# Output weights and residual with their channel means taken off beforehand, and a layer norm that takes the mean of squares alone

## The chip, the core and the metric

The kernel runs on one core of one Trainium2 chip. Its engines: TensorE (PE; PEld is its weight load), VectorE (DVE), ScalarE (ACT), GpSimd (POOL) and SyncE (SP), and 16 DMA engines that serve queues issued from SP, ACT and POOL. PE multiplies into PSUM; DVE and ACT read PSUM; POOL works on SBUF alone. The metric is the device time in microseconds of one execution.

## What is computed

One layer of a hybrid decoder for a prompt of 1024 tokens and 8 sampled tokens (1032 columns in all). The part that the change touches, cut from the reference:

```python
proj = jnp.einsum('ntd,de->nte', x, P['w_in'])
...
gated = jnp.concatenate([o_A * _silu(z_A), o_B * _silu(z_B), o_C * _silu(z_C), o_D * _silu(z_D)], axis=-1)
out = jnp.einsum('nte,ed->ntd', gated, P['w_out'])
y = _layernorm(ALPHA_DN * x + out, P['ln_g'], P['ln_b'])

def _layernorm(x, g, b):
    mu = jnp.mean(xf, axis=-1, keepdims=True)
    var = jnp.mean(jnp.square(xf - mu), axis=-1, keepdims=True)
    return (xf - mu) * lax.rsqrt(var + LN_EPS) * g + b
```

The mean and the variance go over the 2048 channels of one token. `o_A` is a gated delta rule, `o_B` an RWKV-7 recurrence, `o_C` an attention with forget gates (over the prompt, and over paged caches for the sampled tokens), `o_D` a pooling. `w_out` is 2048 by 2048.

## The kernel before, in words

**Layout.** Channels lie on the 128 partitions and tokens on the columns, so the 2048 channels are 16 tiles of 128 by 1032. A product in fp32 precision is three matmuls of rounded halves (`mm3`, lines 306 to 310): weight and data are each split into a rounded value `hi` and a remainder `lo`.

**Weights.** `weight` and `fetch` (lines 280 to 304) load a piece of 128 by 512 (256 KB) into `raw` (two buffers, on ACT's DMA queue), let ACT cast it to `hi` (line 302) and DVE subtract to get `lo` (line 303). They run up to two pieces ahead of the product that asks, with a high priority. For the output pass pieces 48 to 63 are kept in SBUF (`wkh`, `wkl`), all others go through four rotating buffers.

**Order.** The tile framework schedules the instructions: within each engine it orders them by a modelled timeline and by priority, which is the program's order unless a block raises it, and each engine then takes its own queue strictly in order. The kernel's side work is written as Python generators ("fillers") that are advanced by `fill` (lines 315 to 327): a filler with rate 1.3 gets 1.3 steps at each call. `project` (lines 343 to 361) calls it four times for a tile of the input projection; `drain` runs what is left.

**Stages.** (1) The input projection, 57 tiles of 128 output columns, each 144 matmuls of 344 columns. In `inputs` (lines 854 to 881) come first the tiles of branch B, then, from `self.add(self.start_b(), 1)` on (line 878), the sixteen tiles of branch A, the delta rule; beside them run `post_a` and `prep_a` (lines 385 to 488), and `start_b` (lines 1893 to 1897): the inverses of branch B and its step for the sampled tokens, 44 steps. `inputs_cd` then projects the rest beside the inverses of A and the cached scores (`cached`) and the recurrences (`recurrent`). (2) The attention over the prompt (`mixing`), with the cached values beside it. (3) The output product, one pass for each branch in the order D, B, A, C. The first three (`out_pass`, lines 1699 to 1721) add into sixteen accumulators `y`; the third of them also adds 2^0.25 times the residual, loaded from `in_xT` (lines 1711 to 1714).

**The last pass** (`out_last`, lines 1723 to 1781) takes the columns in three groups of 392, 384 and 256. For each group and each of 16 channel tiles PE first multiplies `mneg` (all entries -16/2048) with a rounded copy of `y[0]` (line 1765), then adds twelve matmuls; this takes off an estimate of the mean. DVE adds the PSUM result into `y` (line 1769) and `y` into a running sum `s1` (line 1775); ACT squares (line 1776); POOL, and in the third group DVE, adds the squares into `s2` (line 1777). PSUM has five buffers for these results. When a group is done, `norm` (lines 1736 to 1754) forms the means of `s1` and `s2` by two matmuls with a constant matrix (line 1741), copies them out, subtracts the squared mean and takes the reciprocal root on ACT (`rsqrt`, lines 1231 to 1235). Then for each channel tile DVE or POOL subtracts the mean (line 1750) and multiplies (line 1751), ACT applies scale and shift (line 1752), and SP stores (line 1753). `norm` of one group is a filler beside the matmuls of the next; that of the third group runs alone at the end.

Of the kernel before, what the change touches and what calls it, by code (L numbers as in the profile page):

```python
# [18 lines left out]
G3 = 344  # L19
# [160 lines left out]
class Kernel:  # L180
# [94 lines left out]
    def weights(self, pool, srcs, pieces, keep=1 << 30):  # L275


        self.wp, self.wsrc, self.wraw, self.wsplit, self.wkeep, self.wn = pool, srcs, {}, {}, keep, pieces
# [7 lines left out]
    def fetch(self, i):  # L286
        nc, p = self.nc, self.wn
        w = 4 // p
        for j in range(i // p, min(i // p + 4, len(self.wsrc))):
# [3 lines left out]
            for n in range(p * j, p * j + p):  # L293
# [8 lines left out]
                nc.scalar.copy(hi, raw)  # L302
                nc.vector.tensor_tensor(lo, raw, hi.bitcast(F32), op=ALU.subtract)  # L303
# [1382 lines left out]

    def gated(self, br, gp, stage):
# [11 lines left out]
    def out_pass(self, i, g, stage):  # L1699
# [3 lines left out]
        for ct in range(16):  # L1703
# [7 lines left out]
            if i == 2:  # L1711
                xr = self.t(stage, [128, N], "ostg")
                nc.sync.dma_start(xr, I["xT"][ct])
                nc.vector.scalar_tensor_tensor(y, xr, ALPHA, y, op0=ALU.mult, op1=ALU.add)
# [8 lines left out]
    def out_last(self, i, g, stage, pool):  # L1723


# [4 lines left out]
        mneg = self.t(pool, [128, 128], "mneg", F32R)  # L1730
        nc.vector.tensor_scalar(mneg, m2k, -16.0, None, op0=ALU.mult)
        yr = self.t(stage, [128, N], "ostg", F32R)
        nc.scalar.copy(yr, self.y[0])
        W = {}

        def norm(s, n, st):
            s1, s2 = st
            sq = self.t(pool, [128, GROUPS[0]], "sq", bufs=2)[:, :n]
            for x in (s1, s2):
                ps = self.ps("b", (128, n))  # L1740
                nc.tensor.matmul(ps, lhsT=m2k, rhs=x, start=True, stop=True)
                nc.vector.tensor_copy(x, ps)
            nc.scalar.activation(sq, s1, AF.Square)
            nc.vector.tensor_tensor(s2, s2, sq, op=ALU.subtract)
            self.rsqrt(s2, s2, self.eps["ln"])
            yield True
            for ct in range(16):
                y = self.y[ct][:, s]
                e = nc.gpsimd if ct * NPOOL[n] % 16 < NPOOL[n] and ct else nc.vector
                e.tensor_tensor(y, y, s1, op=ALU.subtract)  # L1750
# [5 lines left out]
        for n in GROUPS:  # L1756
            s = slice(g0, g0 + n)
            st = [self.t(pool, [128, GROUPS[0]], x, bufs=2)[:, :n] for x in ("s1", "s2")]
            for ct in range(16):
# [5 lines left out]
                nc.tensor.matmul(ps, lhsT=mneg, rhs=yr[:, s], start=True, stop=False)  # L1765
                for j in range(4):
                    self.mm3(ps, hi[:, j], lo[:, j], gh[:, j, s], gl[:, j, s], False, j == 3)
                y = self.y[ct][:, s]
                nc.vector.tensor_tensor(y, y, ps, op=ALU.add)  # L1769
                if ct == 0:  # L1770
                    nc.vector.tensor_copy(st[0], y)
                    nc.scalar.activation(st[1], y, AF.Square)
                else:
                    sq = self.t(pool, [128, GROUPS[0]], "sq", bufs=2)[:, :n]
                    nc.vector.tensor_tensor(st[0], st[0], y, op=ALU.add)  # L1775
# [191 lines left out]
```

## Time and profile before

| | |
|---|---|
| median of 3 runs | 2395.63 us (2390.84 to 2396.36) |
| the profiled execution | 2396.94 us, of which the span of the profile 2395.2 us |
| busy: PE, PEld | 2282.6 us (95%), 2023.0 us (84%) |
| busy: DVE, ACT, POOL | 1364.7 us (57%), 938.4 us (39%), 295.0 us (12%) |
| DMA | 402.44 MB, mean 168 GB/s |
| mean granted clock of PE | 0.979 |

Times in the profile count from the first instruction. Matmuls are pipelined, so that the duration of one is longer than the time from its start to the next one's start. A view of windows gives for each stretch its length, the time in which each engine was busy with the number of its instructions in brackets, the granted clock of PE (1.00 is full speed), the mean busy share of the DMA engines and what they moved. A view of waits gives idle time of an engine ahead of a line's instructions, and what ended it.

### The profile page before, as it was taken

The numbers are of one execution on the slowest core, as the hardware profiler recorded it, in microseconds if no ns is written. First come the engines' busy times: TensorE is split into PE (matmuls) and PEld (weight loads), VectorE is DVE, ScalarE is ACT, GpSimd is POOL, SyncE is SP. The second block draws the span as 40 slices with busy tenths as digits, with TensorE's granted clock in tenths as the row PEclk, the third lists the DMA queues.
The fourth block names the chain that finished last, engine by engine and source line by source line (L and its number), as shares of the span: only waits on it lengthen the run. The fifth ranks groups of instructions, "written<-read, shape, count | busy, mean of one in ns | idle before, by whom it ended". The sixth has DMA issues, their size and how long they took to land. (4 is left out here: it accounts for less than half of the span.)

```text
span 2395.2 us, 47251 instructions
## 1 busy us (share of the span) xinstructions
PE 2282.6 (95%) x17640; PEld 2023.0 (84%) x17640; DVE 1364.7 (57%) x2676; ACT 938.4 (39%) x1853; POOL 295.0 (12%) x408
## 2 busy tenths in 40 slices
PE   8999999999899999999999999999899999999984
PEld 8999999998899999787787877899755578889984
DVE  4665757677576557432222245555578644564598
ACT  5644445434454444121111122454366665211244
POOL 0000000000000000103111121100132110100175
PEclk9999999999999999999999999999999999999997
DMA  6133323545523336778878888653488775683212
GB/s 215 56 100 95 104 85 95 151 106 120 113 81 94 89 107 142 172 187 264 274 250 283 259 273 288 232 161 107 124 260 248 223 282 192 219 304 129 88 63 88
DMA packets 369664, 402.44 MB, mean 168 GB/s; under 512 B 204877, under 2 KB 228350, under 8 KB 368666
## 3 DMA queue, kind: packets, MB, share of 16 engines
q1 hardware_dynamic: 307698, 263.83, 37.3%
q10 hardware_dynamic: 50056, 101.60, 13.9%
q0 software_dynamic: 11680, 33.99, 4.3%
q8 instruction: 139, 2.28, 0.4%
q14 instruction: 91, 0.75, 0.1%
HBM read 314.56 MB, written 84.67 MB: 167 GB/s over the span
## 5 line engine op out<-in xcount | busy, mean ns | idle before, releaser
L308 PE MATMUL pj<-xh,wlo 128*128 128x344 f32 x2688 | 873.1, 326 | 16.7 <-DVE wlo L303 8.6
L309 PE MATMUL pj<-xl,whi 128*128 128x344 f32 x2688 | 871.5, 324 | 0.0
L310 PE MATMUL pj<-xh,whi 128*128 128x344 f32 x2688 | 865.2, 324 | 0.0
L308 PEld LDWEIGHTS pj<-xh,wlo 128*128 128x128 f32 x2688 | 508.1, 189 | 37.1 <-issue 11.4
L309 PEld LDWEIGHTS pj<-xl,whi 128*128 128x128 f32 x2688 | 508.5, 189 | 19.8 <-issue 14.4
L310 PEld LDWEIGHTS pj<-xh,whi 128*128 128x128 f32 x2688 | 507.9, 189 | 16.4 <-issue 13.1
L302 ACT CAST whi<-raw 128x256 fp32r<-128x256 f32 (+1 forms) x504 | 213.0, 424 | 732.6 <-PE pj L310 530.2
L303 DVE TENSOR_TENSOR wlo<-raw,whi 128x256 fp32r<-128x256 f32 (+1 forms) x504 | 226.8, 452 | 365.5 <-ACT whi L302 356.1
L309 PE MATMUL o<-gl,whi 128*128 128x344 f32 x576 | 185.8, 323 | 0.0
L308 PE MATMUL o<-gh,wlo 128*128 128x344 f32 x576 | 184.6, 325 | 0.8 <-ACT gh L1695 0.5
L310 PE MATMUL o<-gh,whi 128*128 128x344 f32 x576 | 185.1, 321 | 0.0
L308 PEld LDWEIGHTS o<-gh,wlo 128*128 128x128 f32 x576 | 107.9, 188 | 21.8 <-DVE y L1720 9.4
L309 PEld LDWEIGHTS o<-gl,whi 128*128 128x128 f32 x576 | 109.0, 189 | 2.3 <-DVE ps L1221 0.9
L310 PEld LDWEIGHTS o<-gh,whi 128*128 128x128 f32 x576 | 109.0, 189 | 0.8 <-issue 0.8
L365 ACT ACTIVATE stg<-pj 128x344 f32<-128x344 f32 x168 | 74.6, 457 | 74.2 <-PE pj L310 73.0
L997 PE MATMUL k<-dkv,dqb 128*32 128x256 f32 x1024 | 88.4, 394 | 15.1 <-DMA dkv<-in_ck 9.0
L1720 DVE TENSOR_TENSOR y<-y,o 128x344 f32<-128x344 f32 x96 | 48.0, 510 | 57.3 <-PE o L310 57.0
L1105 PE MATMUL k<-dkv,dpT 128*8 128x512 f32 x512 | 71.5, 635 | 0.8 <-DMA dkv<-in_cv 0.8
L861 DVE TENSOR_TENSOR cpl<-cpt,cph 128x512 fp32r<-128x512 f32 (+1 forms) x96 | 60.9, 653 | 15.7 <-ACT cph L860 14.9
L308 PE MATMUL o<-gh,wkl 128*128 128x392 f32 (+2 forms) x192 | 63.9, 333 | 0.6 <-DVE wkl L303 0.5
L310 PE MATMUL o<-gh,wkh 128*128 128x392 f32 (+2 forms) x192 | 63.6, 331 | 0.0
L309 PE MATMUL o<-gl,wkh 128*128 128x392 f32 (+2 forms) x192 | 63.3, 330 | 0.0
(597 smaller groups left out, 3321.9 us busy)
## 6 DMA issues: line engine op xcount, KB each, us to landing
dkv<-in_ck SPq DMA_DIRECT2D x256, 256.0 KB
dkv<-in_cv SPq DMA_DIRECT2D x256, 256.0 KB
raw<-in_w ACTq DMA_DIRECT2D x228, 256.0 KB
out_pj<-stg ACTq DMA_DIRECT2D x33, 516.0 KB
bop<-bop SPq DMA_DIRECT2D x16, 1024.0 KB
raw<-in_wo ACTq DMA_DIRECT2D x64, 256.0 KB
aop<-aop SPq DMA_DIRECT2D x16, 768.0 KB
aop<-aost SPq DMA_DIRECT2D x40, 256.0 KB
```

The source lines that it names most:

```text
L302: nc.scalar.copy(hi, raw)
L303: nc.vector.tensor_tensor(lo, raw, hi.bitcast(F32), op=ALU.subtract)
L308: nc.tensor.matmul(ps, lhsT=wlo, rhs=xh, start=start, stop=False)
L309: nc.tensor.matmul(ps, lhsT=whi, rhs=xl, start=False, stop=False)
L310: self.last = nc.tensor.matmul(ps, lhsT=whi, rhs=xh, start=False, stop=stop).ins
L365: self.nc.scalar.activation(dst[:, g * G3:g * G3 + G3], ps[g], func)
L861: nc.vector.tensor_tensor(pl[:, off:], pt[:, off:], ph[:, off:].bitcast(F32), op=ALU.subtract)
L997: nc.tensor.matmul(ps[32 * hp:32 * hp + 32], lhsT=qb[:, hp, b], rhs=kt[:, :, hp], start=b == 0, stop=b == 7)
L1105: mm = lambda i: nc.tensor.matmul(po[32 * i:32 * i + 8], lhsT=pTv[:, c, :, 4 * bg + i], rhs=t[i // 2][:, i % 2], start=False, stop=c == 31)
L1720: nc.vector.tensor_tensor(y[:, s], y[:, s], ps[g], op=ALU.add)
```

## The change

`start_b` gets a third part, `centre`, and its rate goes from 1 to 1.3. `centre` loads all output weights and sums them over the output channels (64 pieces, SP queue and DVE), loads the residual and sums it over its channels (POOL, then two matmuls for each third of the columns), loads it a second time, subtracts the mean (POOL) and stores the result in DRAM (`XC`). The 16 columns `wm` hold minus the means of the weights. When the output weights are split later, `wm` is added: ACT's one cast becomes four activations with a bias, DVE's one subtraction four with a scalar. The third output pass reads `XC` instead of `in_xT`. With that the sum over channels of `y` is zero but for rounding, and the last pass leaves out the `mneg` matmuls, the sum `s1` and everything that came from it.

```diff
@@ fetch
-                nc.scalar.copy(hi, raw)
-                nc.vector.tensor_tensor(lo, raw, hi.bitcast(F32), op=ALU.subtract)
+                if self.wless:
+                    m = self.wless(n)
+                    for k in range(4):
+                        nc.scalar.activation(hi[:, k], raw[:, k], AF.Identity, bias=m[:, k:k + 1])
+                        nc.vector.scalar_tensor_tensor(lo[:, k], raw[:, k], m[:, k:k + 1], hi[:, k].bitcast(F32),
+                                                       op0=ALU.add, op1=ALU.subtract)
+                else:
...
@@ new
+    def centre(self, keep):
+        nc = self.nc
+        self.wm = self.t(keep, [128, 16], "wm")
+        with self.tc.tile_pool(reuse_waits="tile", name="cen", bufs=1) as pool:
+            part = self.t(pool, [128, 16, 16], "wpart")
+            load = lambda n: self.t(pool, [128, N], "cin", bufs=2)[:, 0:n]
+            for ct in range(16):
+                for br in range(4):
+                    r = load(512)
+                    nc.sync.dma_start(r.rearrange("p (k m) -> p k m", k=4), self.I["wo"][ct][:, 4 * br:4 * br + 4])
+                    nc.vector.reduce_sum(part[:, 4 * br:4 * br + 4, ct], r.rearrange("p (k m) -> p k m", k=4), axis=AX.X)
+                yield 1
+            nc.vector.reduce_sum(self.wm, part, axis=AX.X)
+            nc.vector.tensor_scalar(self.wm, self.wm, -1.0 / D, None, op0=ALU.mult)
+            xs = self.t(pool, [128, N], "csum")
+            for k in range(16):
+                r = xs if k == 0 else load(N)
+                nc.sync.dma_start(r, self.I["xT"][k])
+                if k:
+                    nc.gpsimd.tensor_tensor(xs, xs, r, op=ALU.add)
+                if k % 4 == 3:
+                    yield 1
+            m2k = self.t(pool, [128, 128], "cone", F32R)
+            nc.vector.tensor_scalar(m2k, self.onec.to_broadcast([128, 128]), 1.0 / D, None, op0=ALU.mult)
+            for g in range(3):
+                s = slice(g * G3, g * G3 + G3)
+                hi, lo = (self.t(pool, [128, N], "cin", F32R, bufs=2)[:, 0:G3] for _ in range(2))
+                nc.scalar.copy(hi, xs[:, s])
+                nc.vector.tensor_tensor(lo, xs[:, s], hi.bitcast(F32), op=ALU.subtract)
+                ps = self.ps("b", (128, G3))
+                nc.tensor.matmul(ps, lhsT=m2k, rhs=lo, start=True, stop=False)
+                nc.tensor.matmul(ps, lhsT=m2k, rhs=hi, start=False, stop=True)
+                nc.vector.tensor_copy(xs[:, s], ps)
+            yield 1
+            for k in range(16):
+                r = load(N)
+                nc.sync.dma_start(r, self.I["xT"][k])
+                nc.gpsimd.tensor_tensor(r, r, xs, op=ALU.subtract)
+                nc.sync.dma_start(self.XC[k], r)
+                if k % 2:
+                    yield 1
@@ out_pass
-                nc.sync.dma_start(xr, I["xT"][ct])
+                nc.sync.dma_start(xr, self.XC[ct])
@@ out_last
-        mneg = self.t(pool, [128, 128], "mneg", F32R)
-        nc.vector.tensor_scalar(mneg, m2k, -16.0, None, op0=ALU.mult)
-        yr = self.t(stage, [128, N], "ostg", F32R)
-        nc.scalar.copy(yr, self.y[0])
...
-        def norm(s, n, st):
-            s1, s2 = st
-            sq = self.t(pool, [128, GROUPS[0]], "sq", bufs=2)[:, :n]
-            for x in (s1, s2):
-                ps = self.ps("b", (128, n))
-                nc.tensor.matmul(ps, lhsT=m2k, rhs=x, start=True, stop=True)
-                nc.vector.tensor_copy(x, ps)
-            nc.scalar.activation(sq, s1, AF.Square)
-            nc.vector.tensor_tensor(s2, s2, sq, op=ALU.subtract)
-            self.rsqrt(s2, s2, self.eps["ln"])
+        def norm(s, n, s2):
+            ps = self.ps("b", (128, n))
+            nc.tensor.matmul(ps, lhsT=m2k, rhs=s2, start=True, stop=True)
+            self.rsqrt(s2, ps, self.eps["ln"])
...
-                e.tensor_tensor(y, y, s1, op=ALU.subtract)
                 e.tensor_tensor(y, y, s2, op=ALU.mult)
...
-                nc.tensor.matmul(ps, lhsT=mneg, rhs=yr[:, s], start=True, stop=False)
                 for j in range(4):
-                    self.mm3(ps, hi[:, j], lo[:, j], gh[:, j, s], gl[:, j, s], False, j == 3)
+                    self.mm3(ps, hi[:, j], lo[:, j], gh[:, j, s], gl[:, j, s], j == 0, j == 3)
...
-                    nc.vector.tensor_copy(st[0], y)
...
-                    nc.vector.tensor_tensor(st[0], st[0], y, op=ALU.add)
@@ inputs
-            self.add(self.start_b(), 1)
+            self.add(self.start_b(cp), 1.3)
@@ start_b
+        yield from self.centre(keep)
```

## Rows read from the trace of the kernel before

**Rows 1.** Windows of the end: length; PE, PEld, DVE, ACT, POOL; PEclk, DMA share, GB/s

```profile
2245.30:2284.80 39.50, 37.99 (x208) 37.01 (x209) 29.03 (x47) 14.75 (x28) 12.47 (x12) 1.00 0.29 94
2284.80:2331.80 47.00, 40.45 (x215) 38.93 (x214) 45.03 (x56) 20.83 (x37) 36.92 (x31) 0.93 0.19 69
2331.80:2369.50 37.70, 29.55 (x213) 28.11 (x211) 36.29 (x58) 16.28 (x31) 25.02 (x21) 0.86 0.23 85
2369.50:2395.20 25.70, 1.92 (x4) 0.80 (x4) 17.60 (x30) 11.92 (x24) 12.10 (x14) 0.58 0.24 82
```

**Rows 2.** The waits of PE from 2280 us to the end: us, times, longest

```profile
PE o L1765 <- DVE y L1769: 14.7, 6, 5.3
PE b L1741 <- DVE s L1777: 8.2, 1, 8.2
```

**Rows 3.** The chain that ended last, 2246 to 2275 us: start, us, what

```profile
2250.62 3.06 DMA raw<-in_wo
...
2270.25 0.70 DVE wkl L303
```

**Rows 4.** PE's timeline at the start of the third group: start, us

```profile
2331.77 0.28 PE L1765 MATMUL o<-ostg,mneg 128*128 128x256 f32 x1
...
2333.30 0.28 PE L1765 MATMUL o<-ostg,mneg 128*128 128x256 f32 x1
```

**Rows 5.** DVE's groups by shape, 2245 us on: busy us, mean ns | idle before

```profile
L1750 DVE TENSOR_TENSOR y<-y,s 128x392 f32<-128x392 f32 x9 | 11.1, 1301 | 0.0
L1751 DVE TENSOR_TENSOR y<-y,s 128x384 f32<-128x384 f32 x7 | 9.1, 1356 | 0.0
...
L1777 DVE TENSOR_TENSOR s<-s,sq 128x256 f32<-128x256 f32 x15 | 7.9, 525 | 0.1
...
L1769 DVE TENSOR_TENSOR y<-y,o 128x256 f32<-128x256 f32 x16 | 6.4, 410 | 0.5 <-PE o L310 0.5
```

**Rows 6.** Groups of ACT's instructions by line and shape, the whole run

```profile
L302 ACT CAST whi<-raw 128x256 fp32r<-128x256 f32 x456 | 183.2, 403 | 583.2 <-PE pj L310 530.2 <-DMA raw<-in_w 20.9 <-DMA dkv<-in_ck 9.9
...
L302 ACT CAST whi<-raw 128x512 fp32r<-128x512 f32 x48 | 29.7, 619 | 149.3 <-PE o L310 130.6 <-DMA raw<-in_wo 10.3 <-DVE y L1720 6.2
...
L555 ACT ACTIVATE bot<-bot,par 128x512 f32<-128x512 f32 x8 | 5.8, 723 | 1.2 <-DVE bot L554 1.2
```

**Rows 7.** The timeline of the tail, from 2379 us: start, duration

```profile
2379.59 1.22 PE L1741 MATMUL b<-s,m2k 128*128 128x256 f32 x2 [8.23 <-DVE s L1777]
...
2381.84 0.51 ACT L1234 ACTIVATE s<-s,epsln 128x256 f32<-128x256 f32 x1 [4.06 <-DVE s L1744]
...
2382.83 6.82 DVE L1751 TENSOR_TENSOR y<-y,s 128x256 f32<-128x256 f32 x9 [1.02 <-ACT s L1235]
```

**Rows 8.** The stores of line 394: ns min/median/max, first and last start

```profile
L394 SPq DMA_DIRECT2D out_pj<-stg x12: 338/360/702, 471.7 to 836.3; - x12
```

**Rows 9.** Windows of earlier stretches

```profile
0.00:36.00 36.00, 27.42 (x165) 27.42 (x166) 22.55 (x36) 21.60 (x30) 1.24 (x6) 1.00 0.87 298
520.00:540.00 20.00, 20.00 (x128) 19.72 (x126) 19.31 (x51) 8.06 (x17) 0.00 (x0) 1.00 0.17 54
700.00:880.00 180.00, 180.00 (x1476) 174.02 (x1475) 109.11 (x193) 86.31 (x169) 0.91 (x4) 1.00 0.31 86
880.00:960.00 80.00, 79.39 (x680) 76.48 (x679) 54.76 (x129) 32.80 (x64) 4.82 (x7) 1.00 0.65 147
1080.00:1500.00 420.00, 405.26 (x4304) 321.09 (x4304) 123.98 (x253) 68.96 (x153) 80.39 (x148) 0.98 0.84 271
```

**Rows 10.** Groups of DVE's and POOL's instructions by line and shape, the whole run

```profile
L789 DVE TENSOR_REDUCE cmx<-b 128x1 f32<-128x512 f32 x24 | 16.4, 686 | 3.8 <-PE b L785 3.5
...
L912 POOL TENSOR_TENSOR cnum<-cnum,cz 128x1024 f32<-128x1024 f32 x4 | 9.8, 2456 | 0.3
```

**Rows 11.** POOL's timeline, 890 to 900 us

```profile
898.38 1.81 POOL L1210 MEMSET ivB<- 128x2048 f32 x1 [98.61 <-DVE am L417]
```

**Rows 12.** The waits of PE, 540 to 1010 us

```profile
PE k L1182 <- DMA ivB<-ut: 4.6, 1, 4.6
```

More of the change, by code (lines that the diff above doesn't have):

```diff
@@ L273, in load_x, with weights @@
             nc.vector.tensor_tensor(self.xl[k], r, self.xh[k].bitcast(F32), op=ALU.subtract)
-    def weights(self, pool, srcs, pieces, keep=1 << 30):
+    def weights(self, pool, srcs, pieces, keep=1 << 30, less=None):
+        self.wless = less
         self.wp, self.wsrc, self.wraw, self.wsplit, self.wkeep, self.wn = pool, srcs, {}, {}, keep, pieces
@@ L301, in fetch @@
                 raw = self.wraw[j][:, w * (n % p):w * (n % p) + w]
-                nc.scalar.copy(hi, raw)
-                nc.vector.tensor_tensor(lo, raw, hi.bitcast(F32), op=ALU.subtract)
+                if self.wless:
[5 more added lines that the diff above has]
+                else:
+                    nc.scalar.copy(hi, raw)
+                    nc.vector.tensor_tensor(lo, raw, hi.bitcast(F32), op=ALU.subtract)
                 self.wsplit[n] = hi, lo
@@ L1757, in out_last @@
             s = slice(g0, g0 + n)
-            st = [self.t(pool, [128, GROUPS[0]], x, bufs=2)[:, :n] for x in ("s1", "s2")]
+            s2 = self.t(pool, [128, GROUPS[0]], "s2", bufs=2)[:, :n]
             for ct in range(16):
@@ L1770, in out_last @@
                 if ct == 0:
-                    nc.vector.tensor_copy(st[0], y)
-                    nc.scalar.activation(st[1], y, AF.Square)
+                    nc.scalar.activation(s2, y, AF.Square)
                 else:
                     sq = self.t(pool, [128, GROUPS[0]], "sq", bufs=2)[:, :n]
-                    nc.vector.tensor_tensor(st[0], st[0], y, op=ALU.add)
                     nc.scalar.activation(sq, y, AF.Square)
-                    (nc.gpsimd if ct <= SPOOL[GROUPS.index(n)] else nc.vector).tensor_tensor(st[1], st[1], sq, op=ALU.add)
+                    (nc.gpsimd if ct <= SPOOL[GROUPS.index(n)] else nc.vector).tensor_tensor(s2, s2, sq, op=ALU.add)
                 self.fill()
-            self.add(norm(s, n, st), 1)
+            self.add(norm(s, n, s2), 1)
             g0 += n
@@ L1795, in build @@
         self.UT = tc.dram_tile([4, 16, 32, 32], F32, name="ut")
+        self.XC = tc.dram_tile([16, 128, N], F32, name="xc")
         self.lfd = tc.dram_tile([8, 32, 1024], F32, name="lfd")
@@ L1830, in build @@
                     order = (3, 1, 0, 2)
-                    self.weights(wp, [self.I["wo"][ct][:, 4 * br:4 * br + 4] for br in order for ct in range(16)], 1, 48)
+                    self.weights(wp, [self.I["wo"][ct][:, 4 * br:4 * br + 4] for br in order for ct in range(16)], 1, 48,
+                                 lambda n: self.wm[:, 4 * order[n // 16]:4 * order[n // 16] + 4])
                     with P(name="g1", bufs=1) as g1:
@@ L1891, in inputs_cd, with start_b @@
         self.drain()
-    def start_b(self):
+    def start_b(self, keep):
         yield from self.inverses("B")
```

## The prediction

> **What bounds the kernel now.** I read the span in windows first. TensorE (PE) is busy nearly everywhere except at the end, so the only stretches in which this change can earn time are those where PE waits, and the only way it can lose time is to make PE wait where it does not today. The last 150 us, cut at the ends of the three column groups of the last pass, are [rows 1]: 39.5, 47.0, 37.7 us and a tail of 25.7 us in which PE has almost nothing. The reader should see the DVE column: 45.0 of 47.0 us and 36.3 of 37.7 us. VectorE (DVE), not PE, sets the second and third group. The waits of PE say the same [rows 2]: 14.7 us for the adds of line 1769, because five PSUM buffers are full and DVE is behind. The first group has another limit, the loading and splitting of the sixteen kept weights: DVE is not full there, and the chain of waits goes load, cast, split, next load [rows 3].
>
> **What leaves the end.** (a) PE: 48 matmuls with `mneg`. Thirteen 256-column matmuls lie between two of them, 2331.77 to 2333.30, so one takes 0.118 us [rows 4]; scaled by columns 0.118, 0.177 and 0.18 us, times 16 each, 7.6 us in all. (b) DVE and GpSimd (POOL): the sums `s1`, the subtraction of the mean, and copies. In the second group's time these are fifteen adds and nine subtractions on DVE, the subtractions alone 11.1 us [rows 5]. I then rebuild each stretch.
>
> First group: limited by weights, so (a) is worth nothing here (if it were not, 2.9 us). Each weight is now four pieces on ScalarE (ACT) and four on DVE. A cast takes 0.403 us for 256 columns and 0.619 us for 512; the line through both gives 0.295 us for 128. A bias column adds about 0.1 us (0.723 for 512 with it) [rows 6]. Four pieces are thus 1.2 us (bias free) to 1.6 us (as read) instead of 0.62. DVE no longer has to wait for the whole cast: its last piece follows ACT's by about 0.35 us instead of 0.70 [rows 3], so a pair of weights, with a load of 3.06 us, turns over in about 4.9 us instead of 4.5. Seven pairs: 3 us lost, 2 us back from the adds that no longer stand between. I take 1 us slower; ends 3 us faster and 4 us slower.
>
> Second group: PE needs 16 x 12 x 0.177 = 34 us and 0.8 us for the reduction. DVE keeps its adds and nine multiplications, at most half of its 45.0 us. I take 36 instead of 47.0: 11 us saved (ends 8 and 12).
>
> Third group: PE 16 x 12 x 0.118 = 22.7 us. DVE: 16 adds at 0.410, 15 at 0.525, 7 multiplications at 1.356 [rows 5], 24 us. The two are level, so some wait stays: 27 instead of 37.7, 10.7 us saved (ends 6 and 13).
>
> Tail: add, square and add of the last tile 1.2 us, matmul 1.22, the two activations 1.0 (2381.84 to 2382.83), multiplications 6.82, the last activations and the last store 5.5 (2389.65 to the end) [rows 7], handoffs 0.6: 16.4, I take 17 instead of 25.7. What goes is the backlog of 8.2 us that PE waits for before the last matmul [rows 2] and the copy and subtraction after it. 8.7 us saved (ends 6 and 10).
>
> Sum of the end: 11 + 10.7 + 8.7 - 1 = 29 us, ends 16 and 39.
>
> **What is added in the middle.** Here the work is large, and all of it must hide beside the projections of the delta rule's sixteen tiles. By the stores of line 394 these tiles finish 26 us apart, the first at about 471 us and the last at about 862 [rows 8]; four calls of fill a tile make one each 6.5 us. The new generator has 44 steps before `centre` and 29 in it; at 1.3 a call, 83 steps fit in the 64 calls, so nothing is left for the drain. `centre` starts after 34 calls, at about 690 us.
> - Transfers: 64 of 256 KB, and 48 of 528 KB, 42 MB. The start of the kernel moves 298 GB/s at a share of 0.87; so these are 123 us of all engines, and 700 to 880 us has 0.31 taken, 124 us free [rows 9]. They fill it to the brim. PE's loss beside full queues: 1080 to 1500 us runs at a share of 0.84, with PE 405.3 of 420 us busy, 3.5% idle; 700 to 880 us has no idle at all. 250 us at 3.5% are 9 us. Ends 0 (PE full, as in 700 to 880) and 15 us.
> - DVE: 64 reductions of 512 columns at 0.686 = 44 us [rows 10], some 5 us for the split of the sum. They read tiles that the SP queue loads; with two buffers a load (3.06) and a reduction allow one each 1.95 us, 125 us against the 80 us that the steps give. What stands behind: on DVE the weight splits, for which PE waits; on SP, whose next load waits for a reduction, the operand loads and stores of `prep_a` (lines 407, 440, 485), for which ACT and the stage buffers wait. The splits run up to two weights ahead, which covers single waits.
> - POOL: 15 adds and 16 subtractions of 1032 columns at 2.46 us for 1024 [rows 10], 76 us on an engine that is idle there (0.91 us busy in 180, [rows 9]). DVE pays beside it: nine subtractions of 392 columns next to POOL's took 1.301 us each [rows 5], where one of 512 columns alone took 0.70 [rows 3]. A two-input DVE operation next to POOL thus runs at about 42%, and 76 us of POOL cost DVE 44 us. The Trainium skill (SBUF — State Buffer, "SBUF: two separate sides") goes further: the port pair that the two share is an exclusive lock, held for the whole instruction, so that the loser stands still until the other has ended. By that rule all 76 us would be lost to DVE; the row shows part of it.
> - So DVE between 690 and 862 us: 104 us of today's work, 49, 44: 197 of 172. The 25 us over find room in 880 to 960, where 25 of 80 are free [rows 9]. That DVE may be this full is no harm in itself: 520 to 540 us has DVE 19.31 and PE 20.00 of 20.
> - Late finish: the load, subtract, store loop of the last part needs some 80 us and is given 40, so `centre` ends near 940. Behind it on POOL, and in the memory that it frees, stand the A inverses, whose first memset is at 898 us [rows 11], and after them the cached attention's scores. PE waited 4.6 us for such a chain of transfers once [rows 12]; I take 4 us, ends 0 and 25 (half of a 50 us shift).
> - Output weights of the first three passes: 48 times 0.6 to 1.0 us more ACT. DVE's four pieces follow them. The casts wait 130.6 us for buffers that PE still reads [rows 6], so nothing; without that cover 29 to 48 us.
> - The residual now comes from a DRAM copy of the same size, written some 1100 us before it is read, by a load in the same place: nothing.
>
> Sum of the middle: 13 us lost, ends 0 and 40.
>
> **The sum.** The profiled execution took 2396.94 us. 2396.9 - 29 + 13 = 2380.9; this execution is 1.3 us above the median of the runs, so 2380 us.
>
> **Rivals.** First, slower: POOL's operations block DVE for their whole length. DVE between 690 and 862 has 104 + 49 + 76 = 229 of 172 us, 57 over; the weight splits are two-input operations and stand behind POOL's, PE waits for them, and if none of the excess finds room later: 2396.9 - 29 + 57 = 2425. It decides from the point where the excess passes 29 us. For it: 1.301 against 0.70. Against: PE full with DVE at 97%, and the partial price above. 15 in 100. (This is what the lock in the Trainium skill, SBUF — State Buffer, "SBUF: two separate sides", would do here.)
>
> Second, no change: the late finish decides. Inverses and scores come 50 us later, half of it shows where the projections end, with the 9 us of the queues: 2396.9 - 29 + 34 = 2402; or the order in which DVE takes its multiplications (nine in one block) keeps most of PE's 14.7 us of waits, 2396.9 - 15 + 13 = 2395. 21 in 100.
>
> Third, all hidden: the middle costs 0 to 3 us, 2396.9 - 29 + 1 = 2369. For it: 180 of 180 us busy with 40% of DVE free. 19 in 100.
>
> The forecast, 2370 to 2389, has 45 in 100. About 0.3%, 7 us, is what a measurement of this kernel can tell from no change: faster is below 2388.4. Forecast and third case give 0.64, the second 0.21, the first 0.15. The range leaves out the far end of the first rival and gains at all the good ends together; it ends at 2406, just past the second rival, and at 2358, 11 us below the third, where the end's saving is near its good end: 2358 to 2406.
>
> **What would show it.** Right: the four windows of the end at about 40, 36, 27 and 17 us; PE's wait for line 1769 mostly gone; no wait of 8 us before the last matmul; in 690 to 940 us PE within 10 us of full, DMA share above 0.8, DVE near 0.9. Wrong: PE waits for the splits of line 303 or their successors in 690 to 940 us (first rival); the inverses or the scores beginning over 30 us later and PE idle between 960 and 1740 (second); or the first group longer than 45 us, the weights' four pieces being dearer than 1.6 us.

## The result, and the profile after

The change made the kernel slower: 2496.02 us (median of 4 runs, 2486.62 to 2500.88) against 2395.99 us of the kernel before beside it, a ratio of 1.042 (95% interval 1.038 to 1.045). The prediction was 2380 us, range 2358 to 2406. The profiled execution took 2486.62 us, span 2484.9 us, 89.7 us more than the one of before.

**The end did what was forecast.** The windows of the last pass after the change, cut as in [rows 1]; columns as there:

```profile
2363.40:2402.00 38.60, 35.58 (x183) 31.89 (x184) 27.04 (x77) 23.57 (x70) 12.36 (x12) 1.00 0.31 97
2402.00:2440.00 38.00, 36.32 (x205) 35.72 (x204) 20.04 (x27) 20.46 (x36) 26.43 (x24) 1.00 0.23 85
2440.00:2468.50 28.50, 25.41 (x196) 24.73 (x194) 19.99 (x35) 17.77 (x34) 12.73 (x11) 0.94 0.31 112
2468.50:2484.90 16.40, 1.13 (x2) 0.41 (x2) 8.41 (x13) 10.12 (x20) 6.15 (x7) 0.56 0.38 128
```

The reader should see the DVE column: 20.0 of 38.0 us where [rows 1] had 45.0 of 47.0. PE is the limit of the second group now. The four stretches add up to 121.5 us instead of 149.9: 28.4 us saved. PE's waits from 2363 us to the end (us, times, longest) answer to [rows 2]:

```profile
PE o L316 <- DVE y L1808: 4.7, 2, 3.1
...
PE b L1785 <- DVE s L1814: 1.9, 1, 1.9
```

The 14.7 us behind DVE's adds are down to 4.7, and the 8.2 us before the last matmul to 1.9. DVE's and ACT's groups by shape, for [rows 5, 6], from 2363 us on; the line of the splits in the first three passes is from the whole run:

```profile
L307 DVE SCALAR_TENSOR_TENSOR wkl<-raw,wm,wkh 128x128 fp32r<-128x128 f32 x64 | 20.8, 377 | 10.9 <-ACT wkh L306 10.9
...
L1814 DVE TENSOR_TENSOR s<-s,sq 128x256 f32<-128x256 f32 x15 | 7.1, 475 | 1.7 <-ACT sq L1813 1.1
```

```profile
L306 ACT ACTIVATE whi<-raw,wm 128x128 fp32r<-128x128 f32 x192 | 61.3, 390 | 131.9 <-PE o L318 112.3 <-DMA raw<-in_wo 7.1 <-PE k L1113 6.3
```

A piece costs ACT 0.39 us, so a weight 1.56 us, the far end of the estimate; the 112.3 us in which these pieces wait for buffers that PE still reads are the cover that was named, and the first three passes (first matmul of a pass to the first kept weight) take 327.6 us (2035.8 to 2363.4) after 326.1 (1920.4 to 2246.5) before. The tail for [rows 7]: start, duration.

```profile
2470.37 1.13 PE L1785 MATMUL b<-s,m2k 128*128 128x256 f32 x2 [1.91 <-DVE s L1814]
...
2472.49 6.81 DVE L1791 TENSOR_TENSOR y<-y,s 128x256 f32<-128x256 f32 x9 [2.17 <-ACT s L1243]
```

**The middle lost 118 us instead of 13** (89.7 + 28.4). The first matmul of the output passes comes at 2035.8 us instead of 1920.4, 115.4 us late. Up to there PE stands still for 168.8 us instead of 68.3, which is 100.5 us of it; the other 14.9 us are longer busy time (1867.0 after 1852.1 us, for about as many matmuls) at a mean granted clock of 0.96 after 0.98. Of the 100.5 us, 94.7 are lost between 700 and 1060 us. Windows of the delta rule's tiles, for [rows 9], and of the stretch that the prediction named for its signs:

```profile
700.00:880.00 180.00, 165.61 (x1252) 159.37 (x1250) 116.66 (x209) 65.70 (x134) 0.91 (x4) 0.97 0.49 148
880.00:960.00 80.00, 52.80 (x296) 49.91 (x296) 28.14 (x38) 11.90 (x30) 36.10 (x15) 0.82 0.56 185
960.00:1060.00 100.00, 38.29 (x379) 34.72 (x380) 67.80 (x71) 35.90 (x60) 44.83 (x21) 0.63 0.71 218
...
940.00:960.00 20.00, 3.68 (x8) 2.08 (x8) 3.60 (x7) 2.91 (x6) 8.80 (x4) 0.50 0.35 119
690.00:940.00 250.00, 224.73 (x1650) 216.50 (x1644) 150.10 (x260) 81.41 (x169) 29.48 (x21) 0.96 0.52 161
```

The row to read is that of 940 to 960 us: PE is busy 3.68 of 20 us, DVE 3.60, ACT 2.91, and the DMA engines stand at a share of 0.35. Only POOL works, 8.80 us, all of it before 951 us. Where no queue is full and one engine off the main path is all that works, the others wait for it in order. The waits from 700 to 1060 us say for what (one fence for each engine: PE, DVE, ACT, SP):

```profile
PE a L471 <- DVE am L462: 27.2, 3, 24.8
PE b L1727 <- DVE cin L1725: 19.7, 3, 17.6
PE pj L316 <- ACT stg L373: 19.5, 4, 9.6
PE a L471 <- DVE aoeg L466: 16.9, 3, 8.2
PE b L1545 <- DVE hsl L1544: 13.6, 4, 5.8
PE pj L316 <- DVE wlo L311: 4.6, 5, 2.1
PE a L487 <- ACT aost L474: 1.8, 1, 1.8
```

```profile
DVE wpart L1707 <- DMA cin<-in_wo: 54.5, 50, 2.4
...
DVE cin L1725 <- ACT cin L1724: 15.6, 1, 15.6
```

```profile
ACT cin L1724 <- POOL csum L1716: 16.1, 1, 16.1
```

```profile
SPq L1706 <- DMA cin<-in_wo: 56.4, 51, 2.9
SPq L1735 <- POOL cin L1734: 42.2, 14, 7.3
SPq L1714 <- POOL csum L1716: 31.1, 13, 2.6
SPq L416 <- DVE aokb L453: 29.8, 4, 21.1
SPq L1706 <- DVE wpart L1707: 25.5, 35, 1.2
...
SPq L1706 <- DMA out_oBS<-sS: 16.4, 1, 16.4
```

PE's seven waits are all of the 103.3 us for which it stands still there: 59.5 us for `prep_a`'s matmuls (lines 471, 487 and 1545), 19.5 us for ACT to empty a tile into a stage buffer (line 373), 19.7 us for the split of the residual's sum (line 1727), and 4.6 us for the splits of the weights (line 311). The 64 reductions of `centre`, over at 900.8 us, wait for their loads fifty times, 54.5 us in all, 2.4 us at most, and behind them on DVE stand the splits and `prep_a`. At 936 to 951 us PE waits for DVE's split of the residual's sum (line 1725), DVE for ACT's cast (1724), and ACT for POOL's sum (1716), whose fifteen adds go from 903.4 to 950.8 us, 36.1 us of them at work and 11.0 waiting for loads: the whole chain in one stretch. DVE's timeline (start, duration, idle before) and, for [rows 11], POOL's:

```profile
951.38 0.52 DVE L1725 TENSOR_TENSOR cin<-csum,cin 128x344 fp32r<-128x344 f32 x1 [15.62 <-ACT cin L1724]
...
970.58 2.85 DVE L480 TENSOR_TENSOR aogb<-aogb,cst 128x512 f32<-128x512 f32 x1
```

```profile
1050.18 2.52 POOL L1734 TENSOR_TENSOR cin<-cin,csum 128x1032 f32<-128x1032 f32 x1 [4.62 <-DMA cin<-in_xT]
1052.64 1.80 POOL L1218 MEMSET ivB<- 128x2048 f32 x1
```

The inverses of branch A, whose memset [rows 11] put at 898 us, start 154 us late. `prep_a`, which makes what they load, is 134.5 us late (its last store, line 493, at 1082.4 us after 947.9). The memset itself begins as POOL ends its last subtraction of `centre`, so that the last part of the 154 us is `centre` standing ahead of it in POOL's queue. Between 934.3 and 1036.8 us PE has no matmul of the projection: those of the residual's sum and of `prep_a` stand ahead in its order. From 960 to 1060 us it is busy 38 of 100 us, at a mean granted clock of 0.63. The stores of the tiles, for [rows 8], are only 21 us late (857.3 after 836.3): the tiles left PSUM nearly in time, and what was late was the work on them.

```profile
L402 SPq DMA_DIRECT2D out_pj<-stg x12: 338/362/616, 472.3 to 857.3; - x12
```

PE's waits for the inverses' transfers (line 1182 in [rows 12], 4.6 us there and 6.9 us in all) are 5.1 us now and only come later.

The groups of `centre` itself are as dear as was worked out from [rows 10] (there 686 ns and, for 1024 columns, 2456):

```profile
L1707 DVE TENSOR_REDUCE wpart<-cin 128x4 f32<-128x512 f32 x64 | 44.0, 687 | 54.7 <-DMA cin<-in_wo 54.5
L1734 POOL TENSOR_TENSOR cin<-cin,csum 128x1032 f32<-128x1032 f32 x16 | 41.5, 2603 | 60.4 <-DMA cin<-in_xT 59.8 <-POOL cin L1734 0.5
L1716 POOL TENSOR_TENSOR csum<-csum,cin 128x1032 f32<-128x1032 f32 x15 | 36.1, 2407 | 93.5 <-DMA raw<-in_w 82.2 <-DMA cin<-in_xT 11.0
```

### The profile page after: what moved, and what is told of

It is laid out like the page before. It is cut to its first block, busy times and chain, and to the rows that moved or that the text cites. A ratio compares the mean times of both kernels' runs of the same rounds, so it can differ in the third digit from the quotient of the medians.

```text
span 2484.9 us, 47826 instructions
## 1 busy us (share of the span) xinstructions
PE 2286.0 (92%) x17592; PEld 2023.5 (81%) x17592; DVE 1414.3 (57%) x2858; ACT 980.4 (39%) x2044; POOL 342.5 (14%) x416
## 4 chain that ended last, share of the span: by engine, by line
PE 41%; DMA 9%; DVE 7%; ACT 2%; SPq 1%; issue 1%; ACTq 0%; DVEq 0%; POOL 0%
PE pj L316 6%; PE pj L318 6%; PE pj L317 6%; PE o L316 4%; PE o L317 4%; PE o L318 4%; PE k L1005 3%; DMA dkv<-in_ck 2%; PE k L1113 2%; DVE y L1791 1%; DMA bop<-bop 1%; DMA raw<-in_wo 1%; DMA dkv<-in_cv 1%; DVE cpl L869 1%; DMA ostg<-xc 1%
## 5 line engine op out<-in xcount | busy, mean ns | idle before, releaser
L310 ACT CAST whi<-raw 128x256 fp32r<-128x256 f32 x456 | 182.8, 404 | 639.1 <-PE pj L318 499.0
L311 DVE TENSOR_TENSOR wlo<-raw,whi 128x256 fp32r<-128x256 f32 x456 | 205.3, 453 | 333.0 <-ACT whi L310 323.2
L306 ACT ACTIVATE whi<-raw,wm 128x128 fp32r<-128x128 f32 x192 | 61.3, 390 | 131.9 <-PE o L318 112.3
L869 DVE TENSOR_TENSOR cpl<-cpt,cph 128x512 fp32r<-128x512 f32 (+1 forms) x96 | 67.7, 724 | 16.5 <-ACT cph L868 15.8
L1707 DVE TENSOR_REDUCE wpart<-cin 128x4 f32<-128x512 f32 x64 | 44.0, 687 | 54.7 <-DMA cin<-in_wo 54.5
```

Source lines behind the costliest of these rows:

```text
L306: nc.scalar.activation(hi[:, k], raw[:, k], AF.Identity, bias=m[:, k:k + 1])
L869: nc.vector.tensor_tensor(pl[:, off:], pt[:, off:], ph[:, off:].bitcast(F32), op=ALU.subtract)
L1707: nc.vector.reduce_sum(part[:, 4 * br:4 * br + 4, ct], r.rearrange("p (k m) -> p k m", k=4), axis=AX.X)
```

## The experiments

My theory after this reading: each engine takes its queue in order, and `centre` put into the queues of SP, DVE, ACT and PE instructions that wait for a load or for POOL; what stands behind (the splits, `prep_a`) waits with them, though no engine is full. Rivals: POOL's operations block DVE; the DMA queues are full; DVE's capacity; the new rate.

### First set: which part of the change costs what

The end alone, the work of `centre` taken out:

```diff
@@ centre
-        with self.tc.tile_pool(reuse_waits="tile", name="cen", bufs=1) as pool:
...
+        nc.vector.memset(self.wm, 0.0)
+        yield 1
@@ out_pass
-                nc.sync.dma_start(xr, self.XC[ct])
+                nc.sync.dma_start(xr, I["xT"][ct])
@@ inputs
-            self.add(self.start_b(cp), 1.3)
+            self.add(self.start_b(cp), 1)
```

> The kernel after without `centre`: the output weights are still split in four pieces with a bias, but the bias is zero, the residual is x itself, and the new generator has its old rate of 1. Left out: the mean over the channels. If all of the 90 us lost comes from `centre` (all theories agree here but one), 2396 - 28 = 2368 us, 2360 to 2376. If the pieces of the output weights in the first three passes cost anything, the time is above 2376; at 0.6 us for each of 48 weights it would be 2397.

Measured: 2368.1 us (before beside it 2400.1; ratio 0.987, 0.983 to 0.991). The end is worth its 28 us, the four pieces cost the passes nothing that can be seen, and all of the loss is `centre` and its rate.

The sums of the output weights alone (all of `centre` from the line `xs = ...` on taken out):

```diff
-            xs = self.t(pool, [128, N], "csum")
...
-                nc.sync.dma_start(xr, self.XC[ct])
+                nc.sync.dma_start(xr, I["xT"][ct])
```

> `centre` with its first part alone: the 64 loads and reductions of the output weights; the residual is x itself (left out: its mean). Head of line (my theory: DVE, SP and POOL take their work in order, and what stands behind a late load of `centre` waits with it): the reductions' waits of 54.5 us hold DVE and cost PE the 18 us seen at 780 to 900 us and part of the hole behind it, 2368 + 20 to 50 = 2388 to 2418. POOL's port lock: no POOL operation is left, so nothing, 2368 to 2375. DVE's capacity: 44 us of reductions remain and most of the loss with them, above 2420.

Measured: 2424.4 us (ratio 1.010, 1.007 to 1.014): 56 us more than the end alone, without any POOL operation of `centre`.

The residual's part alone:

```diff
-            for ct in range(16):
-                for br in range(4):
...
-            nc.vector.reduce_sum(self.wm, part, axis=AX.X)
+            nc.vector.memset(self.wm, 0.0)
```

> `centre` with its second and third part alone: the sum of x, its reduction on TensorE, the subtraction and the stores; the weights' means are zero (left out: the means of the output weights). Head of line: the loads of x on SP with two buffers, each waiting for POOL, and DVE and ACT waiting in order for POOL's sum, 2368 + 40 to 80 = 2408 to 2448. Port lock: 76 us of POOL on DVE's adds, nearly all of the loss, 2440 to 2490. DVE's capacity: little, below 2385.

Measured: 2429.6 us (1.013, 1.006 to 1.019): 61 us more than the end alone. The two parts make 118 of the 128 us that lie between the end alone and the whole change; the new rate, which a run below prices at 11 us, is in both.

All of `centre` but POOL's work:

```diff
-                if k:
-                    nc.gpsimd.tensor_tensor(xs, xs, r, op=ALU.add)
...
-                nc.gpsimd.tensor_tensor(r, r, xs, op=ALU.subtract)
```

> `centre` with all its transfers and reductions, but without POOL's 15 adds and 16 subtractions (left out: the residual's mean). Head of line: the 54.5 us of waits for loads stay, POOL's chain goes, 2368 + 30 to 60 = 2398 to 2428. Port lock: all of it goes, 2368 to 2380. Full DMA queues: the 42 MB are still moved, so nothing is won against the 2496 us of the kernel after: above 2470.

Measured: 2507.5 us (1.045, 1.041 to 1.049), no faster than the whole change. Mine had put part of the loss on POOL's chain and was wrong by that; the port lock, by which all of it goes with POOL's operations, was wrong too. Only full queues had the time right. Against them speak the share of the DMA engines, which is 0.80 and 0.74 at 900 to 940 and 940 to 980 us here while PE has 44 of 80 us ([rows 9] has PE at 405 of 420 us beside 0.84), and a kernel further down that moves all sums' loads and loses 9 us. POOL's work is not free, though. The whole change and this kernel:

```profile
700.00:1060.00 360.00, 256.69 (x1927) 243.99 (x1926) 212.60 (x318) 113.51 (x223) 81.84 (x40) 0.84 0.57 176
700.00:1060.00 360.00, 270.65 (x2007) 259.33 (x2007) 197.65 (x369) 118.35 (x234) 4.26 (x9) 0.85 0.63 183
```

Without POOL's operations PE stands still 14 us less in this stretch, a split of line 311 takes 0.42 us instead of 0.93 (880 to 1060 us), and the inverses begin at 1021.1 us instead of 1052.6. This kernel then loses more after 1060 us (its output passes begin at 2053.9 us, 18.1 later), and why was not found. As each load of x now waits only for the one before it in its buffer, SP goes on holding what stands behind, and the split of x waits in order for a load (15.4 us on ACT) as it did for POOL (16.1).

### Second set: the sums, one queue at a time

The three kernels begin from the sums alone (2424 us). Loads without reductions; loads on POOL's queue; eight buffers:

```diff
-                    nc.vector.reduce_sum(part[:, 4 * br:4 * br + 4, ct], ...
```

> As the kernel with the sums alone (2424 us), its 64 loads kept and its 64 reductions taken away (left out: the means). If DVE is what is held, by reductions that stand before the weight splits and wait for loads, all of the 56 us goes: 2368 to 2375. If SP is what is held, by loads that wait for their buffer while the loads and stores of `prep_a` stand behind them, a buffer is free only when the load before it has landed, so most stays: 2395 to 2424. If it is the transfers themselves on shared queues: as much as before, 2415 to 2430.

Measured: 2406.9 us (8 runs; 1.004, 1.002 to 1.007).

```diff
-                    nc.sync.dma_start(r.rearrange(...
+                    nc.gpsimd.dma_start(r.rearrange(...
```

> As the kernel with the sums alone (2424 us), but its 64 loads are issued by POOL, which has next to nothing to do there, instead of SP; the reductions stay. If SP's order is the cause, the 56 us goes: 2368 to 2380. If DVE's order is the cause, the reductions wait as long as before: 2415 to 2430. If it is the transfers: 2415 to 2430 too.

Measured: 2407.5 us (8 runs; 1.003, 1.001 to 1.005).

```diff
-            load = lambda n: self.t(pool, [128, N], "cin", bufs=2)[:, 0:n]
+            load = lambda n: self.t(pool, [128, n], "cin", bufs=8)
```

> As the kernel with the sums alone (2424 us), with eight buffers of 512 columns for the loads instead of two. A load then waits only for the reduction eight before it, so that neither SP nor DVE is held long: by either order 2368 to 2390, the less the more the order that is laid down lets loads run ahead. By the transfers alone: 2415 to 2430, for they come no slower.

Measured: 2412.1 us (8 runs; 1.006, 1.004 to 1.008). Each removal takes away 12 to 17 of 56 us, and none takes it all. The loads without reductions show how SP's loads hold other engines too. ACT's timeline there (start, duration, idle before; ACTq is its DMA issue):

```profile
789.33 0.34 ACTq L293 DMA_DIRECT2D raw<-in_w  x1
789.76 0.41 ACT L310 CAST whi<-raw 128x256 fp32r<-128x256 f32 x1 [6.33 <-DMA cin<-in_wo]
...
802.22 0.34 ACTq L293 DMA_DIRECT2D raw<-in_w  x1
802.60 0.63 ACT L465 ACTIVATE aoeg<-aoeg 128x512 f32<-128x512 f32 x1 [9.99 <-DMA cin<-in_wo]
```

ACT issues the weight loads, and twice here it stands still for 6 and 10 us before an issue, until a load of `centre` has landed that SP had issued. The two share no data. The built program names the tie: beside DVE, each of the two issues waits for one of eight counters of landed transfers, which the framework hands out in turn to the transfers of SP and ACT alike, and the transfer that brings the counter to the value waited for is a load of `centre`. So an issue on ACT can wait for an older transfer that still stands in SP's queue.

Both removals together, the loads alone and on POOL's queue:

```diff
-                    nc.sync.dma_start(r.rearrange(...
-                    nc.vector.reduce_sum(part[:, 4 * br:4 * br + 4, ct], ...
+                    nc.gpsimd.dma_start(r.rearrange(...
```

> Both single removals together: of the sums alone (2424 us) only the 64 loads are left, and POOL issues them (left out: the means). Loads on SP without reductions gave 2407, loads on POOL with reductions 2408, the rate alone 2379. If the two orders, SP's and DVE's, make the loss between them, each hiding the other's removal, 2368 to 2388. If the transfers themselves slow those of `prep_a` and of the weights, still 2400 to 2410.

Measured: 2387.7 us (8 runs, 2380.0 to 2398.8; 0.995, 0.993 to 0.998). The two removals add up (17 + 17 against 37): DVE's order and SP's order, the counters included, make some 17 to 20 us each. Taking the reductions away also takes their 44 us of work off DVE, so DVE's part is its order and its work together. The expectation had the time right and one word wrong, for neither hid the other.

The rate alone, as an edit of the end alone:

```diff
-            self.add(self.start_b(cp), 1)
+            self.add(self.start_b(cp), 1.3)
```

> The end alone (2368 us), with the new generator's rate of 1.3 in place of 1 and nothing else (left out: the mean over the channels). What the kernels with loads, with loads on POOL's queue and with eight buffers have in common is some 40 us that none of the three changes took away, and the rate. If the rate does it, by bringing the work of the samples forward into the tiles where `prep_a` needs the same engines, 2395 to 2410. If it is the loads and reductions themselves, 2364 to 2374.

Measured: 2379.0 us (6 runs, 2367.8 to 2381.5; 0.990, 0.987 to 0.993): 11 us, between the two theories, with runs at either end of that step. So of the sums' 56 us, 11 are the rate, some 37 the two orders, and 9 (2388 less 2379) are left for the transfers themselves. DVE's capacity was not tested by itself; DVE is busy 117 of 180 us in the whole change.

### Third set: the residual

The transfers of the residual's part on POOL's queue:

```diff
-                nc.sync.dma_start(r, self.I["xT"][k])
+                nc.gpsimd.dma_start(r, self.I["xT"][k])
...
-                nc.sync.dma_start(self.XC[k], r)
+                nc.gpsimd.dma_start(self.XC[k], r)
```

> The residual's part alone (2424 to 2435 us) with its 48 transfers issued by POOL, which works on them anyway, instead of SP (left out: the means of the output weights). If SP's order holds `prep_a`'s loads and stores behind those that wait for POOL, most of the 61 us goes: 2368 to 2395. If it is DVE and ACT that wait in order for POOL's sum, or the transfers, 2410 to 2435.

Measured: 2466.7 us (1.029, 1.025 to 1.034), 37 us worse than on SP. That fell outside both. POOL now issues a load only when it has done with the adds before it:

```profile
775.05 5.03 POOL L1709 TENSOR_TENSOR csum<-csum,cin 128x1032 f32<-128x1032 f32 x2 [3.26 <-DMA cin<-in_xT]
780.04 1.09 POOL L1707 DMA_DIRECT2D cin<-in_xT  x2
785.15 2.40 POOL L1709 TENSOR_TENSOR csum<-csum,cin 128x1032 f32<-128x1032 f32 x1 [4.03 <-DMA cin<-in_xT]
```

Two loads, 3 to 4 us of waiting, two adds, two loads: the sum is ready for ACT's cast at 834.9 us where the kernel on SP's queue had it at 809.6, and all that waits in order for it waits longer. POOL's queue was no way out here, for POOL has a part in the chain.

The sum and its reduction alone; the second load, subtraction and store alone; and both without the split and the matmuls between them:

```diff
-            for k in range(16):
-                r = load(N)
-                nc.sync.dma_start(r, self.I["xT"][k])
-                nc.gpsimd.tensor_tensor(r, r, xs, op=ALU.subtract)
-                nc.sync.dma_start(self.XC[k], r)
```

> The residual's part (2430 us) with the sum of x and its reduction alone: no second load, subtraction or store (left out: both means). Base is the end alone at the same rate, 2379 us. If the loss is ACT, DVE and TensorE waiting in order for POOL's sum: most of the 51 us is here, 2405 to 2430. If it is the transfers in SP's order, it goes by their number, 16 of 48: 2390 to 2400.

Measured: 2420.8 us (1.008, 1.006 to 1.011): 42 us over the rate alone.

```diff
-            for k in range(16):
-                r = xs if k == 0 else load(N)
...
-                nc.vector.tensor_copy(xs[:, s], ps)
+            nc.vector.memset(xs, 0.0)
+            yield 4
```

> The other half: the second load, the subtraction and the store alone, of a sum set to zero (left out: both means). Nothing of ACT, DVE or TensorE waits for this part, but SP's order holds 32 of the 48 transfers and POOL all of the subtractions. In order behind POOL's sum: little, 2379 to 2390. SP's order or the transfers: 2405 to 2425.

Measured: 2390.7 us (9 runs; 0.996, 0.994 to 0.998): 12 us over the rate alone, with twice the transfers.

```diff
-            for g in range(3):
-                s = slice(g * G3, g * G3 + G3)
...
-                nc.vector.tensor_copy(xs[:, s], ps)
```

> The residual's part with all its transfers and POOL operations, but without the split and the matmuls between them, so that ACT, DVE and TensorE have nothing to wait for (left out: the reduction over the partitions, and the means of the output weights). If they are what is held, 2379 to 2400; if SP is, or the transfers, still 2420 to 2435.

Measured: 2404.9 us (9 runs; 1.003, 1.001 to 1.006). So 16 transfers with a result that three engines wait for cost 42 us, 32 transfers for which none waits cost 12, and taking away nine small operations and six matmuls, some 8 us of work in the trace of the whole change, gives back 25. What is left in the last kernel, 26 us over the rate alone, need not be SP's order. Its window of 760 to 820 us, and that of the rate alone:

```profile
760.00:820.00 60.00, 51.28 (x410) 49.50 (x408) 54.57 (x44) 18.43 (x37) 38.10 (x17) 0.97 0.64 192
760.00:820.00 60.00, 60.00 (x480) 58.98 (x479) 34.83 (x60) 29.94 (x59) 0.20 (x2) 1.00 0.32 79
```

Beside POOL's operations DVE does 44 operations in 54.57 us where it does 60 in 34.83 without them; a split of line 311 takes 1.35 us instead of 0.42. DVE is nearly full here. How these 26 us, and the 12 of the other half, divide between that, SP's order and the transfers was not tested. In the sum alone one sees where a backlog turns into lost time (two windows, then PE's and ACT's waits at 840 to 860 us):

```profile
820.00:840.00 20.00, 20.00 (x128) 19.83 (x127) 7.96 (x16) 7.11 (x14) 0.00 (x0) 1.00 0.14 40
840.00:860.00 20.00, 10.99 (x130) 10.60 (x129) 12.28 (x20) 8.51 (x16) 0.10 (x1) 0.74 0.52 120
```

```profile
PE pj L316 <- ACT stg L373: 7.2, 1, 7.2
```

```profile
ACT stg L373 <- DVE am L425: 5.9, 1, 5.9
```

POOL's sum is over by 814 us and PE runs on full; the bill comes 30 us later. `prep_a` is behind, so that the four stage buffers are all still to be read (line 425), ACT cannot empty PSUM into one (line 373), and PE has no bank for the next tile.

### A version of the same idea without the chain

The mean of x comes from the first projection, by a column of 1/2048 in the padding of its weights, so x is neither loaded nor summed for it; one row is loaded back. The weights' sums for output pass n are made during pass n - 1; only the first pass's sixteen loads stay in the delta rule's tiles, with three buffers and loads two ahead.

```diff
+                if p == 2 and j in (0, 2, 4, 6):
+                    nc.gpsimd.memset(self.wraw[j][:, :, 96], 1.0 / D)
...
+                            nc.sync.dma_start(self.xm, self.O["pj"][MISC, 96].partition_broadcast(128))
...
+        for ct in range(16 + lead):
+            if ct < 16:
+                r.append(buf())
+                nc.sync.dma_start(r[ct], self.I["wo"][ct][:, 4 * br:4 * br + 4])
+            if ct >= lead:
+                nc.vector.reduce_sum(part[:, :, ct - lead], r[ct - lead], axis=AX.X)
```

> A version of the same idea with next to nothing in the delta rule's tiles: the mean of x comes out of the first projection, by a column of 1/D in the padding of its weights; only the sixteen loads for the first output pass stay there (three buffers, two loads ahead, rate 1), the sums for each later pass are made during the pass before it; the residual's mean is taken off in the first output pass by DVE, in place of ACT's copy. If what is in the delta rule's tiles is the cause, a quarter of the sums costs at most a quarter of 56 us there and the end keeps its 28: 2368 + 0 to 14, and 0 to 6 in the passes: 2368 to 2388. If the output passes have no room for 48 loads and DVE's 24 us more, above 2395.

Measured: 2397.8 us (10 runs; 0.999, 0.997 to 1.001), no better than before. The middle was 9 us late, and the passes took 349 us. At their start, with the load of the mean and the first sums ahead of what PE needs:

```profile
1930.00:1950.00 20.00, 16.51 (x85) 12.46 (x87) 10.21 (x13) 9.27 (x17) 6.84 (x5) 0.77 0.83 282
1950.00:1970.00 20.00, 11.96 (x57) 9.27 (x53) 11.15 (x24) 5.68 (x13) 2.14 (x4) 0.66 0.93 323
```

The same with that work some tiles later in the pass:

```diff
+        yield 4
+        for ct in range(16):
+            self.nc.vector.scalar_tensor_tensor(self.y[ct], xm, -ALPHA, self.y[ct], op0=ALU.mult, op1=ALU.add)
+            yield 1
...
+        yield 6 * (br == 1)
+        for ct in range(16 + lead):
```

> As the version with the sums made late (2398 us, whose middle ended 9 us later than that of the end alone, and whose output passes took 347 us against 326), but the sums for the second pass begin after four tiles of the first, and the mean of x is taken off by one DVE operation a tile four tiles behind ACT's copies, so that neither the first adds nor the first weights wait for a transfer. The 12 us of PE's waits at 1930 to 1970 us should go, 8 of the other 9 stay: 2380 to 2390. If what the passes lose is not at their start but the loads beside the cached values' loads: 2392 to 2400.

Measured: 2387.1 us (10 runs; 0.996, 0.994 to 0.998). The second of the two windows has PE full again:

```profile
1950.00:1970.00 20.00, 20.00 (x129) 18.84 (x128) 13.95 (x27) 11.45 (x30) 2.14 (x4) 1.00 0.86 299
```

A second set of the same kernel:

> The version with the sums made later, once more, beside the next: 2387 us, 2380 to 2394.

Measured: 2388.0 us (6 runs; 0.996, 0.994 to 0.998). Beside it, with the first sixteen loads on POOL's queue, where nothing of this generator needs POOL:

```diff
-                nc.sync.dma_start(r[ct], ...
+                (nc.gpsimd if br == 3 else nc.sync).dma_start(r[ct], ...
```

> The version with the sums made later, its first sixteen loads issued by POOL instead of SP. If what is left of the middle's loss (the output passes begin some 5 us later than with the end alone) is SP's order, 2 to 6 us less than the version beside it; if it is the reductions, the transfers or the jitter of the middle, the same.

Measured: 2375.9 us (4 runs, 2366.6 to 2381.1; 0.991, 0.989 to 0.994), 12 us less than its neighbour and more than was expected. In the profiled execution, the fastest of the four (2366.6 us), the output passes begin at 1916.5 us, before the 1920.4 of the kernel before. This version beats both kernels.

```profile
700.00:880.00 180.00, 177.51 (x1451) 170.23 (x1451) 115.47 (x206) 85.13 (x167) 9.54 (x20) 1.00 0.39 108
```

## Why the prediction was wrong

- **The end: right.** Saved 28.4 us for 29. By stretch: 38.6 for 40.5, 38.0 for 36, 28.5 for 27, 16.4 for 17. The misses are up to 2 us with both signs, so that the sum is within 1 us is partly luck. That PE would take over in the second group, and that the backlog before the last matmul would go, shows in the waits.
- **The first three passes and the residual's load: right**, 1.5 us for nothing, with the cover that was named.
- **The works' own prices: right.** The reductions took 44.0 us for 44, POOL's operations 77.6 for 76, the loads one in 2.1 us (764 to 900 us) for 1.95.
- **The step that failed** is the one on DVE's and SP's order, which ends with "The splits run up to two weights ahead, which covers single waits." It listed what stands behind a waiting reduction and a waiting load, the splits and `prep_a`, and then priced neither: 9 us was the loss beside full queues, taken from 1080 to 1500 us, and the queues were not what was short (share 0.49 and 0.56, not the brim that was worked out). For the splits the cover held, PE waited 4.6 us for them. It does not cover `prep_a`: fifty waits of about 1 us in DVE's queue and as many in SP's put it behind by more than its four stage buffers hold, and PE stood still 59.5 us for its matmuls and 19.5 us for a stage buffer. The split of the residual's sum was counted as "some 5 us" of DVE and not as a wait for POOL that DVE, ACT and PE all take in their order; PE waited 19.7 us for it, and it was worth 25 us in the last set.
- **The start: late.** `centre` was to begin at about 690 us and end near 940. Its first load was issued at 761.1 us, after SP had waited 16.4 us for the store `out_oBS` of branch B's samples, and its last subtraction ended at 1052.7 us. What the late start itself costs is not shown.
- **The late finish: right in kind, wrong by size.** It was given 4 us, at most 25; the second rival gave 34. The inverses came 154 us later, not 50, which is that rival's sign. But PE had lost most of its time by then, waiting for `prep_a` and the sum; its waits for the inverses' transfers did not grow.
- **The signs of being right did not come.** From 690 to 940 us PE is 25 us short of full, the DMA share is 0.52 and DVE is busy 0.60 of the time, where within 10 us, above 0.8 and near 0.9 were named.
- **The first rival: its mechanism is there, but it does not carry the loss.** An operation of 0.69 us took 2.85 us at 970 us, about the time of one POOL operation beside it. The Trainium skill (SBUF — State Buffer, "SBUF: two separate sides") says that the loser of the shared port pair stands still until the other has ended; this row agrees, better than the partial price that I took from [rows 5]. But the sums alone lose 56 us without POOL's operations, and the whole change without them was no faster. What the lock costs in the residual's part, where DVE is nearly full beside POOL, stays open.
- **The rate** was only used to count steps; as a change by itself it cost 11 us.

What stays open: the rate alone and each part's loss over it give 2379 + 45 + 51 = 2475 against 2496 us, so 21 us are of both parts together. How SP's loss divides between its order and the shared counters was not parted, as POOL's queue removes both. That the sums alone leave 9 us for the transfers is a difference of medians whose runs spread by that much. And it was not found where the kernel without POOL's operations loses, after 1060 us, what it had won.

## What to carry to other kernels

Work that "fits" by busy time still has to fit by order: for every instruction added to a shared queue, ask what it waits for, how often, and how much slack the work behind it has (here four stage buffers). Put added loads several steps ahead of their use, on a queue whose engine has no part in the chain, and keep an engine on which the main loop depends from waiting for a slow side sum. Better still, get the number from work that is done anyway: a spare column of a product gave the mean of x without a load or a sum of x.

## What the runs showed that was not expected

- Transfers issued by SP and ACT are tied to each other by shared counters: ACT stood 10 us before a weight load until a transfer of SP had landed.
- The same POOL queue made 64 loads of weights 17 us cheaper and 16 of them 12 us, but the residual's 48 transfers 37 us dearer; in these POOL also computes with what it loads.
- With POOL adding beside it, DVE took 1.35 us for a split of 0.42 us, and 54.6 of 60 us for fewer operations than it otherwise does in 34.8.
- A delay shows late: with the sum alone PE was full again at 820 to 840 us, after the sum that held the others had ended at 814, and then lost 9 of 20 us.
